# Dilated attention in a written order on three engines, value products of two blocks merged, gate and up interleaved by slice: two layers of a hybrid decoder on one core

## The chip, the core and the metric

The kernel runs on one core of one Trainium2 chip. The time is the device time of one execution in microseconds (us). The figure compared is the median of several runs. Beside these there is one profiled execution, from which every row of the trace below comes; rows name lines of the kernel before the change (L1090 is its line 1090).

## The reference, cut to what matters

Two decoder layers over 512 positions of width 1024, all in float32. Each layer is a half-step SwiGLU, a token mixer and another half-step SwiGLU; every one of these six sub-layers sits between two RMS norms with shift, scale and gate taken from `c`. The mixer of layer 0 is latent attention (MLA, 16 heads, causal in blocks of 128). The mixer of layer 1 is dilated attention: three groups of 16 heads with dilations 1, 4 and 16, whose results are weighted by their log-sum-exps.

```python
def swiglu(h, w_gate, w_up, w_down):
    return (jax.nn.silu(h @ w_gate) * (h @ w_up)) @ w_down
...
for g, (window, dilation) in enumerate(DIL_GROUPS):
    o, lse = strided_window_attention(
        proj[:, :, g, 0], proj[:, :, g, 1], proj[:, :, g, 2],
        dilation, window // dilation, rel_bias[:, g * DIL_HEADS:(g + 1) * DIL_HEADS])
    outs.append(o)
    lses.append(lse)
alpha = jax.nn.softmax(jnp.stack(lses, axis=0), axis=0)
o = jnp.sum(alpha[..., None] * jnp.stack(outs, axis=0).astype(jnp.float32), axis=0)
return o.astype(h.dtype).reshape(B, S, DIL_WIDTH) @ w_o
```

## The kernel before

**Dense products.** Every float32 product with a weight is done as three products of split operands (`mm3`, L143 to L145): a raw weight tile comes by DMA (`raw`, 5 buffers), ScalarE (ACT) rounds it to a high part (`whi`, L128, 6 buffers), VectorE (DVE) subtracts to get the low part (`wlo`, L130, in two halves), and TensorE (PE) adds high*high, high*low and low*high. A weight slice is 128x128; a full moving operand has 512 columns. In the trace one such matmul is one record; a plain float32 matmul (transposes, scores, value products) shows as two records.

**Gate and up.** `gate_up_mm` runs the eight 128-wide slices `k` of the gate product, then the eight of the up product, into two PSUM banks. At the start of a sub-layer the first three units (`head`) run on half the positions (256 columns), while VectorE, ScalarE and GpSimd still make the slices of the modulated input (`modulate`, L305 to L307).

**MLA.** For each pair of heads `c` and block `i`, `score`, `turn` (transposes, L890) and `weigh` (value products, L904) pass through a pipe: in one step the kernel emits the scores of block i, the transposes of block i-2 and the value products of block i-3. Other products (`BESIDE`) fill the steps.

**Dilated stage.** `Dil.rest` works on eight pairs of heads. While pair p is attended, the nine projection tiles of pair p+1 (`tile`, 24 matmuls each) run, in the order `ORDER`; their place n = 0 to 8 counts the slots of a pair. In the slots stand:

- n = 0 to 3: `scores(p, n)`. Scores contract over 64 rows: the two heads of a pair use the two halves of the array's rows at once (L1090), each into its own bank. VectorE adds the bias, takes row minima and empties the bank (`tensor_tensor_reduce`, L1103).
- after n = 3: `tops` sends minima through DRAM to bring them into another order; at n = 4, `exps` takes all exponentials on ScalarE (L1155), then `norm` and `norm_out` send the sums through DRAM (L1182 to L1188).
- n = 6 to 8 and n = 0, 1 of the next pair: `mix`, that is `turn` of step 0 to 3 (PE transposes at L1210 with copies on VectorE at L1214; step 3 is a transpose on VectorE, L1206) and `weigh` of the step before. `weigh` (L1235) gives each head 64 of the array's columns; at its last step VectorE multiplies by the reciprocal sums (L1245).
- after each value tile: its transposes (`later`, L1065, copy at L1067) one slot on.

There are two pools of four PSUM banks: `mm` for dense products and scores, `aux` for transposes and value sums.

**What sets the order.** The code records operations; outside a `manual_schedule` block a scheduler of the tile layer places each engine's instructions by readiness and priority. Inside `manual_schedule(engines=...)` the named engines keep the order in which the code is written. In the dilated stage before, only its last part is written by hand (PE and DVE). Each engine runs its queue in order.

Of the kernel before, what the change touches and what calls it, by code (L numbers as in the profile page):

```python
# [7 lines left out]
F32 = mybir.dt.float32  # L8
# [4 lines left out]
PE, ACT, DVE, SP = (getattr(mybir.EngineType, n) for n in ("PE", "Activation", "DVE", "SP"))  # L13

P = 128
SEQ = 512
# [6 lines left out]
PART = 3  # L23
# [9 lines left out]
SPARE = (2, 3)  # L33
TURN = 26
START = 4
HT = SEQ // 2
TT = SEQ // P

# [482 lines left out]
class Ffn:  # L521
# [178 lines left out]
class Mla(Mixer):  # L700
# [148 lines left out]
    def attend(self, c, i, pipe):  # L849
# [48 lines left out]
        def weigh(i):  # L898
            if i == 0:
                box["o"] = t.bank("aux")  # L900
            for j in range(i + 1):
                for e in range(2):
                    h = 2 * c + e
                    nc.tensor.matmul(  # L904
                        box["o"][64 * e : 64 * e + 64, i * P : (i + 1) * P],
                        self.v[j, h // 8][:, (h % 8) * 64 : (h % 8) * 64 + 64],
                        box[i][e][:, j * P : (j + 1) * P],
                        start=i == j == 0,
                        stop=i == j == 3,
                        skip_group_check=True,  # L910
                    )
            if i == 3:
                self.put_o(box["o"])

        pipe.push(i, score, turn, weigh)

# [26 lines left out]
class Dil(Mixer):  # L943
# [124 lines left out]

            self.later = turn

    def scores(self, p, u):
        t, nc = self.t, self.t.nc
        if u == 0:
            self.pairs.pop(p - 2, None)
            self.pairs[p] = {
                "bias": [self.bias_of(2 * p + e) for e in range(2)],
                "m": t.tmp.tile([P, 3, 4, 2], F32, tag="dm", name="dm", bufs=2),
                "z": t.tmp.tile([P, 3, 4, 2], F32, tag="dz", name="dz", bufs=2),
                "y": {},
            }  # L1080
# [3 lines left out]
        s = [t.bank() for _ in range(2)]  # L1084
        y = [t.t("sq", SB) if u < 2 else t.t("u", UB) for _ in range(2)]
        at = 0
        for i, k0, n, b0 in blocks:
            for e in range(2):
                rows = slice(64 * e, 64 * e + 64)
                nc.tensor.matmul(  # L1090
                    s[e][:, at : at + n],
                    q[rows, i * P : (i + 1) * P],
                    k[rows, k0 : k0 + n],
                    start=True,
                    stop=True,
                )
            at += n
        for e in range(2):
            pair["y"][u, e] = y[e]
            at = 0  # L1100
            for i, k0, n, b0 in blocks:
                c = slice(at, at + n)
                nc.vector.tensor_tensor_reduce(  # L1103
                    y[e][:, c],
                    s[e][:, c],
                    pair["bias"][e][:, b0 : b0 + n],
                    -0.125,
                    3e38,
                    ALU.add,
                    ALU.min,  # L1110
                    accum_out=pair["m"][:, g, i, e : e + 1],
                )
                at += n
        if u == 3:
            self.tops(pair)

    def natural(self, dram, src):

# [2 lines left out]
        for a in range(4):  # L1121
            nc.sync.dma_start(
                dram[1].rearrange("(l a j) v -> a l j v", a=4, j=4)[a], src[32 * a : 32 * a + 32, 2]
            )

    def tops(self, pair):
        t, nc = self.t, self.t.nc
        m = pair["m"]
        m0 = t.dram.tile([2, SEQ, 2], F32, tag="m0", name="m0", bufs=2)
        t0 = t.dram.tile([SEQ, 2], F32, tag="t0", name="t0", bufs=2)  # L1130
        self.natural(m0, m)
        x = t.tmp.tile([P, 2, 4, 2], F32, tag="x4", name="x4", bufs=2)
        nc.sync.dma_start(x, m0.rearrange("g (p r) v -> p g r v", r=4))
        top = t.tmp.tile([P, 3, 4, 2], F32, tag="y4", name="y4", bufs=2)
        nc.vector.tensor_tensor(top[:, 1], x[:, 0], x[:, 1], ALU.min)
        nc.vector.tensor_tensor(top[:, 1], top[:, 1], m[:, 1], ALU.min)
# [5 lines left out]
            )  # L1142
        pair["top"] = top

    def exps(self, p):
        nc = self.t.nc
        pair = self.pairs[p]
        for u, (g, blocks) in enumerate(self.BLOCKS):
            for e in range(2):
                y = pair["y"][u, e]  # L1150
                at = 0
                for i, k0, n, b0 in blocks:
# [8 lines left out]
                        accum_out=pair["z"][:, g, i, one],  # L1161
                    )
                    at += n
        self.norm(pair)
        if p < 7:
            self.norm_out(pair)

    def norm(self, pair):
        t, nc = self.t, self.t.nc
# [26 lines left out]
    )  # L1196

    def turn(self, p, step):
        t, nc = self.t, self.t.nc
        _, tag, pieces, _ = self.TURNS[step]  # L1200
        y = self.pairs[p]["y"]
        out = self.pairs[p][step] = []
        for e in range(2):
            x = t.t(tag)
            if pieces is None:
                nc.vector.transpose(x, y[3, e])  # L1206
            else:
                b = t.bank("aux")
                for c, (u, j) in enumerate(pieces):
                    nc.tensor.transpose(  # L1210
                        b[:, c * P : (c + 1) * P], y[u, e][:, j * P : (j + 1) * P], t.ident
                    )
                n = len(pieces) * P
                nc.vector.tensor_copy(x[:, :n], b[:, :n])  # L1214
            out.append(x)

    def weigh(self, p, step, first=0, last=3):
        t, nc = self.t, self.t.nc
# [26 lines left out]
            nc.vector.tensor_tensor(x, pair["acc"], pair["r"], ALU.mult)  # L1245
            self.of.append(x)

    def mix(self, p, step):
        if step < 4:
            self.turn(p, step)  # L1250
        if step:
            self.weigh(p, step - 1)

    def rest(self):
        t = self.t
        t.gates(self)
        self.of = []
        self.tables()
        for u in self.ORDER[6:]:
            self.tile(0, u, 0, SEQ)  # L1260
# [24 lines left out]
        for x in self.of[PART:]:  # L1285
            self.put_o(x)
        self.exps(7)
# [128 lines left out]
```

## Time and profile before

| what | value |
|---|---|
| median of 3 runs | 2275.35 us (2274.54 to 2275.74) |
| the profiled execution | 2273.08 us, its span 2271.3 us |
| busy share of the span: PE, DVE, ACT, POOL | 99%, 53%, 38%, 5% |
| latent attention, 446 to 582 us: busy PE, DVE, ACT | 134.58, 92.02, 100.92 us of 136.00 |
| one pair of the dilated stage, mean of three: busy PE, DVE, ACT | 62.25, 25.52, 24.35 us |

The profiled execution is 2.27 us (0.1%) below the median. Rows of the timeline give start, duration, engine, line, operation, output and inputs, shape (rows*columns of the array, then the moving operand), and count. Matmuls overlap in the pipeline, so durations of neighbours overlap too: what one costs is the distance from its start to the next start.

### The profile page before, as it was taken

How to read it: one execution, taken by the hardware profiler on the slowest of the kernel's cores; microseconds unless marked ns; L12 is line 12 of the kernel's file. 1: busy time of each engine (PE TensorE's matmuls, PEld its weight loads, DVE VectorE, ACT ScalarE, POOL GpSimd, SP SyncE). 2: the span in 40 equal slices, each digit the busy share in tenths (PEclk: the TensorE clock that was granted, in tenths of full speed). 3: DMA queues.
4: the chain of work that ended last, by engine and by line, in shares of the span. 5: the costliest groups of instructions: out<-in, count | busy, mean ns of one | idle time of the engine just before them, and what ended most of it. 6: DMA issues, size and time to landing. Idle time of an engine off the chain costs nothing. (4 is left out here: it accounts for less than half of the span.)

```text
span 2271.3 us, 30190 instructions
## 1 busy us (share of the span) xinstructions
PE 2240.5 (99%) x11422; PEld 1851.4 (82%) x11422; DVE 1203.6 (53%) x2712; ACT 861.3 (38%) x1752; POOL 105.2 (5%) x143
## 2 busy tenths in 40 slices
PE   7999999999999999999999999999999999999998
PEld 5888888877898888898888888778878878888887
DVE  7666566677655366474554473334434367243344
ACT  4422135577633132353222352444344346332232
POOL 0000001210110000020000010000000002000000
PEclk9999999999999999999999999999999999999999
DMA  8575662311255365344653523333333332243231
GB/s 307 163 249 180 187 232 68 100 48 57 76 171 180 93 213 173 106 140 127 191 174 114 156 93 105 80 96 87 81 93 87 89 79 80 75 130 100 76 111 38
DMA packets 121224, 284.04 MB, mean 125 GB/s; under 512 B 44130, under 2 KB 48501, under 8 KB 121078
## 3 DMA queue, kind: packets, MB, share of 16 engines
q1 hardware_dynamic: 121078, 282.11, 40.8%
q8 instruction: 89, 1.46, 0.3%
q14 instruction: 57, 0.47, 0.1%
HBM read 279.67 MB, written 2.39 MB: 124 GB/s over the span
## 5 line engine op out<-in xcount | busy, mean ns | idle before, releaser
L143 PE MATMUL mm<-s,whi 128*128 128x512 f32 (+1 forms) x2116 | 796.9, 377 | 3.5 <-ACT whi L128 2.4
L144 PE MATMUL mm<-s,whi 128*128 128x512 f32 (+1 forms) x2116 | 790.9, 374 | 0.0
L145 PE MATMUL mm<-s,wlo 128*128 128x512 f32 (+1 forms) x2116 | 790.5, 374 | 0.0
L128 ACT ACTIVATE whi<-raw 128x1024 fp32r<-128x1024 f32 (+1 forms) x356 | 369.7, 1053 | 962.2 <-PE mm L144 446.6
L130 DVE TENSOR_TENSOR wlo<-raw,whi 128x512 fp32r<-128x512 f32 (+1 forms) x712 | 465.6, 693 | 397.8 <-ACT whi L128 393.8
L143 PEld LDWEIGHTS mm<-s,whi 128*128 128x128 f32 x2116 | 398.7, 188 | 83.4 <-issue 7.0
L145 PEld LDWEIGHTS mm<-s,wlo 128*128 128x128 f32 x2116 | 398.7, 188 | 70.9
L144 PEld LDWEIGHTS mm<-s,whi 128*128 128x128 f32 x2116 | 398.9, 188 | 68.1
L143 PE MATMUL mm<-whi,s 128*128 128x512 f32 x848 | 332.4, 392 | 1.8 <-ACT s L694 1.1
L144 PE MATMUL mm<-wlo,s 128*128 128x512 f32 x848 | 330.4, 390 | 0.0
L145 PE MATMUL mm<-whi,s 128*128 128x512 f32 x848 | 330.1, 390 | 0.0
L165 DVE CUSTOM_DVE_ANT_0 raw<-raw,cs 128x1024 f32<-128x1024 f32 x130 | 159.9, 1234 | 117.7 <-DMA raw<-w_mod 117.2
L143 PEld LDWEIGHTS mm<-whi,s 128*128 128x128 f32 x848 | 159.2, 188 | 36.3 <-issue 2.5
L145 PEld LDWEIGHTS mm<-whi,s 128*128 128x128 f32 x848 | 159.2, 188 | 33.4 <-issue 0.3
L144 PEld LDWEIGHTS mm<-wlo,s 128*128 128x128 f32 x848 | 159.3, 188 | 32.6 <-issue 0.3
L569 DVE TENSOR_TENSOR gg<-silu,mm 128x512 f32<-128x512 f32 (+1 forms) x95 | 60.3, 635 | 171.5 <-PE mm L145 168.3
L459 DVE TENSOR_TENSOR s<-mm,s 128x512 f32<-128x512 f32 x112 | 76.5, 689 | 125.8 <-PE mm L145 125.6
L318 POOL TENSOR_TENSOR mv<-mv,mhalf 128x1 f32<-128x1 f32 x48 | 36.0, 752 | 1498.0 <-DVE mv L317 1495.5
L570 ACT ACTIVATE s<-gg 128x512 fp32r<-128x512 f32 (+1 forms) x97 | 57.4, 591 | 62.0 <-DVE gg L569 62.0
L567 ACT ACTIVATE silu<-mm 128x512 f32<-128x512 f32 (+1 forms) x95 | 51.5, 543 | 31.9 <-PE mm L145 31.9
L1055 ACT ACTIVATE s<-mm 128x512 f32<-128x512 f32 (+3 forms) x156 | 46.2, 373 | 34.8 <-PE mm L145 34.8
L463 ACT ACTIVATE s<-mm 128x512 f32<-128x512 f32 x40 | 23.8, 595 | 85.8 <-PE mm L145 85.5
(168 smaller groups left out, 1737.3 us busy)
## 6 DMA issues: line engine op xcount, KB each, us to landing
raw<-w_gu SPq DMA_DIRECT2D x168, 512.0 KB, 4.3
raw<-w_mod SPq DMA_DIRECT2D x130, 512.0 KB, 4.8
raw<-w_down SPq DMA_DIRECT2D x88, 512.0 KB, 4.3
raw<-dil_in SPq DMA_DIRECT2D x70, 512.0 KB, 3.6
s<-w_mod SPq DMA_DIRECT2D x28, 256.0 KB, 6.3
raw<-w_gu SPq DMA_DIRECT2D x16, 256.0 KB, 3.6
raw<-mla_o SPq DMA_DIRECT2D x8, 512.0 KB, 3.7
raw<-dil_o SPq DMA_DIRECT2D x8, 512.0 KB, 3.6
```

The lines of the kernel that those rows point to most:

```text
L128: self.nc.scalar.activation(hi, raw, AF.Copy)
L130: self.nc.vector.tensor_tensor(lo[:, r], raw[:, r], f(hi[:, r]), ALU.subtract)
L143: mm(out, w[0], m[0], start=first, stop=False)
L144: mm(out, w[0], m[1], start=False, stop=False)
L145: mm(out, w[1], m[0], start=False, stop=last)
L165: nc.vector.tensor_tensor_reduce(raw, raw, self.cs, 1.0, 0.0, ALU.mult, ALU.add, accum_out=t[:, 0:1])
L318: nc.gpsimd.tensor_tensor(v[:, 1:2], v[:, 0:1], self.mhalf[:, 0:1], ALU.pow)
L459: nc.vector.tensor_tensor(y, b, y, ALU.add)
L567: nc.scalar.activation(s, banks[0], AF.Silu)
L569: nc.vector.tensor_tensor(v, s, banks[1], ALU.mult)
L570: nc.scalar.activation(ghi, v, AF.Copy)
L1055: nc.scalar.activation(out, src, AF.Copy)
```

## The change

- `gate_up_mm` swaps its loops: slice `k` outside, gate and up inside.
- In MLA, `weigh` does nothing for even blocks (but for taking the bank at block 0) and at odd blocks runs the products of the block before and of its own.
- In the dilated stage, PE, ACT and DVE follow the written order. Scores of a pair go into two slots: u = 0 and 1 at n = 0, u = 2 and 3 at n = 1 (u = 3 into `aux` banks). Value products go into the same two slots of the next pair: steps 0 and 1 at n = 0, steps 2 and 3 at n = 1. `turn` is split into the transposes (`turn_up`) and the copies (`turn_down`); steps 0 and 1 are at n = 7 and 8, step 2 at n = 0.
- `tops` is split: the DMAs out and in (`tops_out`) stay with the scores, the VectorE part runs at n = 3. Exponentials are spread over n = 4 to 6, `norm` follows at n = 6, `norm_out` at the end of n = 8. Bias tables are loaded at n = 6 of the pair before.
- `ahead` loads and splits weight tiles `LEAD` = 5 places ahead, the first tiles of the output weights among them.

```diff
+LEAD = 5
...
-        for g in range(2):
-            for k in ks:
+        for k in ks:
+            for g in range(2):
                 t.mm3(
...
             if i == 0:
                 box["o"] = t.bank("aux")
+            elif i % 2:
+                for q in (i - 1, i):
+                    products(q)
+            if i == 3:
+                self.put_o(box["o"])
+
+        def products(i):
             for j in range(i + 1):
...
-    def exps(self, p):
+    def exps(self, p, us):
...
+    def slot(self, p, n):
+
+        if n == 0:
+            if p:
+                b = self.turn_up(p - 1, 2)
+                self.values(p - 1, (0, 1))
+            self.scores(p, 0)
+            self.scores(p, 1)
+            if p:
+                self.turn_down(p - 1, 2, b)
+                self.turn(p - 1, 3)
+        elif n == 1:
+            if p:
+                self.values(p - 1, (2, 3))
+            self.scores(p, 2)
+            self.scores(p, 3, "aux")
+        elif n == 6:
+            self.biases(p + 1)
+        elif n > 6:
+            self.turn(p, n - 7)
+
+    def beside(self, p, n):
+        if n == 3:
+            self.tops(self.pairs[p])
+        elif n == 4:
+            self.exps(p, (2,))
+        elif n == 5:
+            self.exps(p, (0, 1))
+        elif n == 6:
+            self.exps(p, (3,))
+            self.norm(self.pairs[p])
...
-        for p in range(7):
-            for n, u in enumerate(self.ORDER):
-                if n < 4:
-                    self.scores(p, n)
-                if n < 2 and p:
-                    self.mix(p - 1, 3 + n)
-                if n == 4:
-                    self.exps(p)
-                if n >= 6:
-                    self.mix(p, n - 6)
-                if p == 6 and n == 8:
+        with t.tc.manual_schedule(engines={PE, ACT, DVE}):
+            for at, (p, u) in enumerate(tiles):
+                n = self.ORDER.index(u)
+                if p:
+                    self.slot(p - 1, n)
+                if (p, n) == (7, 8):
                     self.scores(7, 0)
-                self.tile(p + 1, u, 0, SEQ)
+                self.ahead(at + LEAD)
+                if p:
+                    self.beside(p - 1, n)
+                self.tile(p, u, 0, SEQ)
+                if p and n == 8:
+                    self.norm_out(self.pairs[p - 1])
         self.later()
+        b = self.turn_up(6, 2)
+        self.values(6, (0, 1))
+        self.turn_down(6, 2, b)
+        self.turn(6, 3)
         self.scores(7, 1)
         for x in self.of[:PART]:
             self.put_o(x)
-        self.mix(6, 3)
         t.new_y()
-        for j in range(PART):
-            self.out_weights(j)
         self.scores(7, 2)
-        self.mix(6, 4)
+        self.values(6, (2, 3))
         self.scores(7, 3)
+        self.tops(self.pairs[7])
```

The order of instructions, at three places. First PE at slot n = 0 of a pair in the dilated stage, before (L1065 are transposes of a value tile, L1090 scores, L1235 value products, L143 to L145 the projection tiles):

```order
L145 MATMUL mm<-s,wlo 128x512
L1065 MATMUL aux<-ident,s 128x128 x4
L1090 MATMUL mm<-s 128x128 x2
L1090 MATMUL mm<-s 128x256 x2
L1235 MATMUL aux<-silu,s 64x128 x8
L143 MATMUL mm<-s,whi 128x512
L144 MATMUL mm<-s,whi 128x512
```

The same place after the change (lines of the changed kernel: L1071 value transposes, L1218 transposes of exponentials, L1252 value products, L1096 scores, L144 to L146 the tiles):

```order
L146 MATMUL mm<-s,wlo 128x512
L1071 MATMUL aux<-ident,s 128x128 x4
L1218 MATMUL aux<-ident,u 128x128 x8
L1252 MATMUL aux<-silu,s 64x256 x4
L1252 MATMUL aux<-gg,s 64x256 x2
L1252 MATMUL aux<-gg,s 64x128 x2
L1096 MATMUL mm<-s 128x128 x2
L1096 MATMUL mm<-s 128x256 x6
L144 MATMUL mm<-s,whi 128x512
```

The scores of u = 1 and the value products of steps 0 and 1 have come into this slot from n = 1, 7 and 8, and step 2's value products have left it for n = 1.

Second PE in MLA between two steps, before (L862 scores, L890 transposes, L904 value products):

```order
L145 MATMUL mm<-whi,s 128x512
L862 MATMUL mm<-s 128x512 x2
L890 MATMUL aux<-ident,u 128x128 x4
L904 MATMUL aux<-silu,s 64x128 x2
L862 MATMUL mm<-s 128x128 x2
L890 MATMUL aux<-ident,sq 128x128 x6
L904 MATMUL aux<-gg,s 64x128 x4
L143 MATMUL mm<-s,whi 128x512
```

and after (L863, L891 and L912 are the same three):

```order
L146 MATMUL mm<-whi,s 128x512
L863 MATMUL mm<-s 128x512 x2
L891 MATMUL aux<-ident,u 128x128 x4
L863 MATMUL mm<-s 128x128 x2
L891 MATMUL aux<-ident,sq 128x128 x6
L912 MATMUL aux<-silu,s 64x128 x2
L912 MATMUL aux<-gg,s 64x128 x4
L144 MATMUL mm<-s,whi 128x512
```

The products of the even block have moved behind the next step's scores and transposes, to those of the odd block.

Third DVE ahead of slot n = 0 after the change (L1073 is the copy of a value tile, L1192 to L1194 are `norm_out`, L1109 empties the score banks, each reduction followed by the reading of its minimum):

```order
L1073 COPY s<-aux 128x512
L1192 TENSOR_TENSOR w_13075<-x_12934 128x4x2
L1193 TENSOR_TENSOR w_13075<-w_13075,dz 128x4x2
L1194 RECIPROCAL w_13075<-w_13075 128x8
L1109 ISA sq,dm<-mm,s 128x128
L1109 ISA dm 128x1
L1109 ISA sq,dm<-mm,s 128x256
```

Before, these three stood ahead of a STREAM_TRANSPOSE, copies and splits of weights, which came before the reductions; now the reductions of slot 0 are directly behind them.

More of the change, by code (lines that the diff above doesn't have):

```diff
@@ L1075, in scores @@
             self.pairs[p] = {
[L1076 removed]
+                "bias": self.bias.pop(p),
                 "m": t.tmp.tile([P, 3, 4, 2], F32, tag="dm", name="dm", bufs=2),
@@ L1083, in scores @@
         q, k = self.qkv[p, 3 * g], self.qkv[p, 3 * g + 1]
-        s = [t.bank() for _ in range(2)]
+        s = [t.bank(tag) for _ in range(2)]
         y = [t.t("sq", SB) if u < 2 else t.t("u", UB) for _ in range(2)]
@@ L1114, in scores, with biases @@
         if u == 3:
-            self.tops(pair)
+            self.tops_out(pair)
+    def biases(self, p):
+        self.bias[p] = [self.bias_of(2 * p + e) for e in range(2)]
     def natural(self, dram, src):
@@ L1246, in weigh, with values, ahead @@
             self.of.append(x)
[L1248 to L1252, printed above, removed]
+    def values(self, p, steps):
+        for n in steps:
+            self.weigh(p, n)
+    def ahead(self, n):
+        while self.coming and self.ahead_of < n:
+            p, u = self.coming.pop(0)
+            self.ahead_of += 1
+            if p == "out":
+                self.out_weights(u)
+            else:
+                self.wt[p, u] = self.t.weights(self.t.a["dil_in"][p, u])
+    def slot(self, p, n):
[27 more added lines that the diff above has]
+            self.norm(self.pairs[p])
     def rest(self):
```

65 lines of the change are left out of this document (36 added, 29 removed).

## The prediction

> **What bounds the kernel now.** I read the page first, then PE's waits, then the timeline of PE in the stages that the change touches.
>
> ```profile
> PE 2240.5 (99%) x11422; PEld 1851.4 (82%) x11422; DVE 1203.6 (53%) x2712; ACT 861.3 (38%) x1752; POOL 105.2 (5%) x143
> ```
>
> PE is busy in 99% of the span. So time can go only if PE waits less or if its own stream becomes shorter. The waits:
>
> ```profile
> PE mm L377 <- DVE s L371: 5.3, 4, 3.3
> PE mm L143 <- DVE dm L1103: 0.7, 1, 0.7
> ```
>
> The longest, 5.3 us, is in the first 20 us, which the change hardly touches. The only wait on the score reductions in the whole run is one of 0.7 us, after the last pair. The next rows are windows, with the busy times of PE, weight load, DVE, ACT and POOL, the granted clock, and the DMA: MLA, then one pair of the dilated stage:
>
> ```profile
> 446.00:582.00 136.00, 134.58 (x842) 99.00 (x840) 92.02 (x281) 100.92 (x239) 16.62 (x23) 1.00 0.16 48
> 1546.44:1608.64 62.20, 62.20 (x347) 49.70 (x346) 25.48 (x83) 24.36 (x76) 0.35 (x2) 1.00 0.35 89
> ```
>
> The pair takes 62.20 us, PE is busy in all of it at the full clock, DVE in 25.48, ACT in 24.36. Written order on DVE and ACT can therefore win nothing there by itself; what counts is what PE's stream costs. "Busy" does not say that the stream is dense, so I look at the distance from start to start. First a slot with scores alone, then one with transposes alone:
>
> ```profile
> 1539.14 0.39 PE L144 MATMUL mm<-s,whi 128*128 128x512 f32 x1
> 1539.37 0.39 PE L145 MATMUL mm<-s,wlo 128*128 128x512 f32 x1
> 1539.68 1.16 PE L1090 MATMUL mm<-s 64*128 64x128 f32 x16
> 1540.78 0.50 PE L143 MATMUL mm<-s,whi 128*128 128x512 f32 x1
> 1541.11 0.39 PE L144 MATMUL mm<-s,whi 128*128 128x512 f32 x1
> ...
> 1563.77 0.40 PE L145 MATMUL mm<-s,wlo 128*128 128x512 f32 x1
> 1564.00 1.08 PE L1210 MATMUL aux<-ident,sq 128*128 128x128 f32 x8
> 1564.84 0.48 PE L143 MATMUL mm<-s,whi 128*128 128x512 f32 x1
> 1565.15 0.40 PE L144 MATMUL mm<-s,whi 128*128 128x512 f32 x1
> ```
>
> A dense matmul takes 0.23 us (1539.14 to 1539.37). From the last one before the scores to the second one after them are 1.74 us; without the scores it would be two steps, 0.46. The 16 score records cost 1.28. They run two by two, one head on each half of the rows, so they are 8 steps of 128 columns. The 8 transposes, also 8 steps of 128 columns but on the whole array (128*128), cost 1565.15 - 1563.77 - 0.46 = 0.92. So a block of work with 64 rows costs 0.36 us more than the same steps on the whole array. The neighbours show where: 0.31 instead of 0.23 from L145 to L1090, and 0.33 from L143 to L144 after it. **Changing the shape in which the array is used costs time on each side.** The tail of the stage gives a second price, from blocks that follow each other:
>
> ```profile
> 1838.94 1.16 PE L1090 MATMUL mm<-s 64*128 64x128 f32 x16
> 1840.03 1.09 PE L1235 MATMUL aux<-gg,s 128*64 128x128 f32 x16
> 1841.06 1.16 PE L1090 MATMUL mm<-s 64*128 64x128 f32 x16
> ```
>
> Score blocks (64*128) and value blocks (128*64) in a chain take 1.09 and 1.03 us, with one change each in place of two: 1.28 - 1.06 = 0.22 per change. From the other side 0.36 / 2 = 0.18. I take 0.20 us per change, with 0.18 and 0.23 as bounds.
>
> [...]
>
> **The change part by part.** *Dilated stage.* Going through PE's order before and after, I count the places where it passes between whole array, 64 rows and 64 columns: 113 before, 57 after. Per pair: before, n = 0 and 1 hold scores and value products (3 changes each), n = 2 and 3 scores alone, n = 7 and 8 value products alone (2 each), 14 in all; after, only n = 0 and 1 (3 each). Eight fewer in seven pairs make the 56. The same number of matmuls runs. 56 x 0.20 = **11.2 us less** (10.1 to 12.9).
>
> *MLA.* Value products stand between whole-array work; the scores there use 96 rows. Two steps, without and with value products:
>
> ```profile
> 451.95 0.39 PE L145 MATMUL mm<-s,wlo 128*128 128x512 f32 x1
> 452.18 1.45 PE L862 MATMUL mm<-s 96*128 96x384 f32 x4
> 453.47 0.38 PE L890 MATMUL aux<-ident,sq 128*128 128x128 f32 x2
> 453.61 0.47 PE L143 MATMUL mm<-whi,s 128*128 128x512 f32 x1
> 453.93 0.39 PE L144 MATMUL mm<-wlo,s 128*128 128x512 f32 x1
> ...
> 482.70 0.40 PE L145 MATMUL mm<-s,wlo 128*128 128x512 f32 x1
> 484.22 0.38 PE L890 MATMUL aux<-ident,sq 128*128 128x128 f32 x2
> 484.53 1.09 PE L904 MATMUL aux<-gg,s 128*64 128x128 f32 x16
> 485.56 0.50 PE L143 MATMUL mm<-whi,s 128*128 128x512 f32 x1
> 485.89 0.39 PE L144 MATMUL mm<-wlo,s 128*128 128x512 f32 x1
> ```
>
> 3.19 - 1.98 = 1.21 us for 16 value records, again 8 steps: 0.29 above the transposes, 0.15 per change at the least. L145 to L862 takes the plain 0.23, so 96 rows count as the whole array. 32 blocks of value products become 18, 28 changes go: 28 x 0.20 = **5.6 us less** (4.1 to 6.4). Products of even blocks come one step later and keep their transposed operand (`silu`, two buffers) longer; the copies that need the buffer wait for PE products which stand right behind the transposes, and are used two steps later, so I put that at nothing; ACT and DVE are busy 74% and 68% there (100.92 and 92.02 of 136), and the cost if that cover is short is below, with the first rival.
>
> *The new slot n = 0.* Here four `mm` banks fill at once, and the next tile wants the first of them again. Before, one tile lay between two score pairs. DVE empties a bank thus:
>
> ```profile
> 1838.02 0.42 DVE L1103 CUSTOM_DVE_ANT_0 sq<-mm,s 128x256 f32<-128x256 f32 x1
> 1838.37 0.08 DVE L1103 DVE_READ_ACCUMULATOR2_ANT dm<- 128x1 f32 x1
> ...
> 1842.23 0.29 DVE L1103 CUSTOM_DVE_ANT_0 u<-mm,s 128x128 f32<-128x128 f32 x1
> 1842.44 0.29 DVE L1103 CUSTOM_DVE_ANT_0 u<-mm,s 128x128 f32<-128x128 f32 x1
> ```
>
> A step takes 0.35 us for 256 columns and 0.21 for 128; the first bank holds one of each, 0.56, and 0.1 for the last read: 0.65. PE's part: u = 0 is 2 + 4 steps of 128 columns, u = 1 is 8 more, 0.11 each (0.92 / 8), with a change ahead and behind 1.5 + 0.2 = 1.7 us to the next tile. The first bank is written after some 5 steps and a matmul's 0.4 of latency (the durations shown), about 1.0, and free at 1.65. It is a close race: 0 to 0.1 us per pair if DVE comes at once. Behind these reductions DVE has two copies and two transposes (0.6 each) for products that run a tile later. I take 0.5 us for seven pairs (0 to 2).
>
> *Other moves.* Exponentials spread over three slots lie beside tiles of 24 x 0.23 = 5.5 us each; ACT then does at most one weight split, 8 exponentials and the emptying of a tile in a slot, and a late emptying hurts only after three more tiles have taken banks. Weight DMAs are issued as far ahead as the buffers allow in both. Bias loads move ahead of use. All beside PE: nothing.
>
> *Tail.* Transposes and products of step 2, 0 and 1 of pair 6 leave n = 7 and 8 and stand behind the last tile. There DVE, not PE, sets the pace: PE's 0.7 us of waiting on it, quoted first, ends that chain. DVE gets two copies and two transposes more in that stretch, 4 x 0.6, and `norm_out`'s 0.5: the wait is over 2.9 us later counted from the last tile, which itself ends some 2.6 us earlier because the work left. And one change fewer in the chain wins nothing there. **0.6 us more** (0 to 1.5).
>
> *Slice-major gate and up.* In steady state the same matmuls at the same pitch; both banks are ready together, and the next unit but one needs them 11 us later. At a sub-layer's start PE waits for slices:
>
> ```profile
> 983.72 0.42 DVE L307 TENSOR_TENSOR s<-u,s 128x256 fp32r<-128x256 f32 x1
> 984.19 0.39 PE L144 MATMUL mm<-s 128*128 128x256 f32 x1 [0.19 <-DVE s L307]
> ```
>
> PE goes on when the low half of the last slice lands. In both orders 47 matmuls stand between the head's first and that one, so the interleaving lets PE wait later, not less: **0** (2 us either way, the four waits of such a start being 1.3 us here).
>
> Sum: -11.2 - 5.6 + 0.5 + 0.6 = -15.7. Against the profiled execution (span 2271.3, with 1.8 us around it 2273.1) that is 2257.4; the median before, 2275.35, is 2.3 us above that, so I predict 2275.35 - 15.7 = **2259.6 us** (-0.7%).
>
> **Rivals.** *Emptying eats part of it.* If a DVE operation of 0.65 us stands in the way at both slots of each pair, PE waits 14 x 0.65 = 9 us, and 2268.7 remains. For it: the race above is close. Against it: in the written order nothing but three small operations stands directly ahead of the reductions. [...] MLA's ACT, at 74%, would have the same effect on a smaller scale.
>
> *The price is not one of changes.* If the 0.3 us belong to each block's first records whatever stands before, merging keeps most of them; with the two costs above 2274 to 2277 results. Against it: blocks in a chain are cheaper, 1.06 against 1.28.
>
> *Slower.* `norm_out` now stands directly ahead of the reductions of slot 0 in DVE's queue and waits for sums that go through DRAM; a late sum would hold the reductions, the banks and so PE.
>
> ```profile
> 1442.70 0.19 ACT L1155 ACTIVATION_READ_ACCUMULATOR u<-u,y 128x1 f32 x1
> 1449.04 0.17 DVE L1182 TENSOR_TENSOR w<-x 128x8 f32<-128x8 f32 x1 [1.32 <-DMA x<-z]
> ...
> 1397.17 5.82 SPq L981 DMA_DIRECT2D s<-tv  x12
> ```
>
> That way took 6.2 us before. After, exponentials end in the tile of n = 6, and `norm_out` is wanted some 14 us later. With the twelve bias loads (5.8 us of issuing) now ahead in the queue it is 12. It decides from 14 us on; at 18 us PE would lose 4 us in each of seven pairs, and the time would be 2259.6 + 28 = 2287.6.
>
> **How the numbers follow.** The forecast (2254 to 2264) gets 0.70, emptying 0.15 (2264 to 2270), no price of changes 0.08, slower 0.07. The forecast's bounds are 10.1 + 4.1 - 2 - 1.5 and 12.9 + 6.4 less nothing, with up to 2 us from the starts: -8.7 to -21.3 at the extremes, hardly all at once. The range 2254 to 2268.5 holds the forecast and most of the first rival, about 0.8. By over 0.2% (4.6 us, about what a measurement can tell from no change): faster 0.85, same 0.08, slower 0.07.
>
> **What would show it.** One pair of the dilated stage near 60.5 us in place of 62.2, PE still busy in all of it, and slots n = 2, 3, 7 and 8 without a 64-wide block; MLA 5 us shorter. A wait of PE's tile (the mm3 after the scores) on the reductions would show the first rival, DVE waiting on x<-z the last one. I am wrong if the pair is shorter by clearly more or less than 1.6 us with no wait of PE in it, for then the price is not what I read.

## The result and the profile after

| | before | after |
|---|---|---|
| median | 2274.95 us (2274.54 to 2275.74, 4 runs) | 2260.96 us (2258.17 to 2261.21, 4 runs) |
| the profiled execution | 2273.08 us, its span 2271.3 | 2258.17 us, its span 2256.1 |

The ratio is 0.9935, with a 95% interval of 0.9918 to 0.9953: 14.0 us less (10.7 to 18.7). The forecast was 15.7 less (2259.6). Rows of after name its own lines; what they are called before is said where it matters.

First the page of after, its line of busy times, and the rows of PE's waits that answer to those of before (engine, what waits, what for; us in total, times, longest):

```profile
PE 2224.4 (99%) x11422; PEld 1853.9 (82%) x11422; DVE 1196.9 (53%) x2712; ACT 848.9 (38%) x1752; POOL 107.9 (5%) x143
```

```profile
PE mm L378 <- DVE s L372: 5.3, 4, 3.3
...
PE mm L144 <- DVE dm L1109: 1.6, 1, 1.6
...
PE mm L144 <- ACT s L695: 1.2, 1, 1.2
```

The same 11422 matmuls now keep PE busy for 16.1 us less, at the same 99%. What went was not waiting but length of PE's own stream. The one wait on the score reductions (L1109, before L1103) has grown from 0.7 to 1.6 us; it is still a single one, at the tail, and none stands in a slot.

Then windows of after: MLA, and two pairs of the dilated stage (columns as in the prediction):

```profile
446.00:577.00 131.00, 129.30 (x826) 98.44 (x826) 91.39 (x280) 99.93 (x239) 16.78 (x24) 1.00 0.16 49
1506.01:1566.47 60.46, 60.46 (x347) 50.08 (x346) 25.40 (x83) 24.29 (x75) 0.20 (x1) 1.00 0.35 90
1566.47:1626.93 60.46, 60.46 (x347) 50.08 (x346) 25.39 (x83) 24.29 (x75) 0.20 (x1) 1.00 0.37 98
```

A pair takes 60.46 us; the prediction asked for "near 60.5 us in place of 62.2, PE still busy in all of it". Slot n = 0 in the timeline of after, PE and then DVE:

```profile
1513.98 1.08 PE L1252 MATMUL aux<-silu,s 128*64 128x256 f32 x8
1514.89 0.82 PE L1252 MATMUL aux<-gg,s 128*64 128x256 f32 x8
1515.64 1.79 PE L1096 MATMUL mm<-s 64*128 64x128 f32 x16
1517.36 0.50 PE L144 MATMUL mm<-s,whi 128*128 128x512 f32 x1
1517.70 0.39 PE L145 MATMUL mm<-s,whi 128*128 128x512 f32 x1
```

```profile
1516.60 0.29 DVE L1109 CUSTOM_DVE_ANT_0 sq<-mm,s 128x128 f32<-128x128 f32 x1 [2.17 <-PE mm L1096]
1516.82 0.08 DVE L1109 DVE_READ_ACCUMULATOR2_ANT dm<- 128x1 f32 x1
1516.82 0.42 DVE L1109 CUSTOM_DVE_ANT_0 sq<-mm,s 128x256 f32<-128x256 f32 x1
1517.16 0.08 DVE L1109 DVE_READ_ACCUMULATOR2_ANT dm<- 128x1 f32 x1
```

Value products, then scores, then the next tile, in one go. The race for the first score bank is as close as the prediction reckoned: the bank is empty at 1517.16 + 0.08 = 1517.24, and PE asks for it at 1517.36. It is won by 0.12 us, with no wait.

To find where the rest of the time went I divide each trace at records that all kernels have: the first score of MLA, the first transposes of the sub-layer behind it, the first score and the last value product of the dilated stage, the end. Every stretch is the difference of two starts in the trace (us). The last column is the mean period of five pairs, taken at the transposes of value tiles. Taken at the first scores of the pairs it is 62.22 before and the same 60.46 after, because the order before shifts a little from pair to pair.

| kernel | to MLA | MLA | middle | dilated | rest | pair |
|---|---|---|---|---|---|---|
| before | 447.65 | 156.87 | 796.06 | 468.01 | 402.67 | 62.17 |
| after | 447.95 | 152.62 | 796.04 | 456.41 | 403.07 | 60.46 |
| e1_slice | 447.98 | 158.44 * | 796.04 | 467.87 | 402.34 | 62.16 |
| e2_mla | 448.85 * | 154.26 * | 796.05 | 468.28 | 403.60 | 62.24 |
| e3_dil | 447.55 | 158.50 * | 796.05 | 456.41 | 402.19 | 60.46 |
| e4_four_visits | 447.86 | 154.19 * | 796.06 | 462.43 | 403.53 | 61.31 |
| e5_alternate | 448.06 | 154.23 * | 796.06 | 460.68 | 402.58 | 61.18 |
| e6_tail | 449.09 * | 154.22 * | 796.07 | 456.24 | 403.36 * | 60.46 |
| e7_last_pair | 447.81 | 154.54 * | 796.06 | 456.40 | 403.05 | 60.46 |
| e9_copies_first | 448.19 | 154.20 * | 796.06 | 461.41 | 402.61 | 61.28 |
| e10_norm_early | 447.88 | 154.24 * | 796.06 | 459.02 * | 403.21 * | 60.46 |
| e11_mla_cover | 447.80 | 152.92 | 796.04 | 458.04 * | 402.91 | 60.46 |
| e12_turn3_first | 449.17 * | 154.20 * | 796.03 | 458.02 | 403.02 | 60.73 |
| e13_tail_order | 447.86 | 154.17 * | 796.06 | 454.34 | 402.66 | 60.46 |

So the change took 4.25 us from MLA and 11.60 from the dilated stage; the start, the middle and the rest moved by 0.7 together, up. The middle repeats within 0.04 us in all kernels, and the dilated stage within 0.01 us in those that share its code in the written order (e3_dil, e7_last_pair). Stretches with a star hold some 3.4 us at half clock; at MLA they come and go with the same code. Windows of before and of e3_dil, whose code up to there is the same (the third number from the end is the granted clock):

```profile
449.00:453.00 4.00, 4.00 (x18) 3.25 (x19) 1.61 (x8) 3.97 (x12) 0.95 (x2) 1.00 0.32 127
```

```profile
449.00:453.00 4.00, 4.00 (x12) 3.20 (x13) 1.62 (x8) 3.83 (x11) 0.85 (x2) 0.57 0.29 111
```

In 449 to 453 us before ran 18 matmul records at clock 1.00, e3_dil 12 at 0.57. The step from the second to the third score of MLA is 1.5 to 1.6 us longer in all eleven profiles with a star at MLA, and equal to 0.01 us in the three others. I subtract that step where I compare MLA.

### The profile page after: what moved, and what is told of

Read it like the earlier page. It is cut to its first block, busy times and chain, and to the rows that moved or that the text cites. A ratio compares the mean times of both kernels' runs of the same rounds, so it can differ in the third digit from the quotient of the medians.

```text
span 2256.1 us, 30214 instructions
## 1 busy us (share of the span) xinstructions
PE 2224.4 (99%) x11422; PEld 1853.9 (82%) x11422; DVE 1196.9 (53%) x2712; ACT 848.9 (38%) x1752; POOL 107.9 (5%) x143
## 4 chain that ended last, share of the span: by engine, by line
PE 92%; issue 2%; ACT 2%; DVE 2%; DMA 1%; POOL 1%; SPq 0%; POOLq 0%; DVEq 0%; ACTq 0%
PE mm L144 28%; PE mm L145 28%; PE mm L146 28%; PE mm L863 1%; PE aux L1252 1%; PE mm L1096 1%; PE aux L1218 1%; PE aux L912 1%; POOL mv L319 1%; PE aux L891 1%; PE aux L513 1%; PE aux L1071 0%; ACT whi L129 0%; DVE x L500 0%; DMA d<-w 0%
## 5 line engine op out<-in xcount | busy, mean ns | idle before, releaser
L144 PE MATMUL mm<-s,whi 128*128 128x512 f32 (+1 forms) x2116 | 793.9, 376 | 2.7 <-ACT whi L129 2.4
L146 PE MATMUL mm<-s,wlo 128*128 128x512 f32 (+1 forms) x2116 | 790.0, 373 | 0.0
L145 PE MATMUL mm<-s,whi 128*128 128x512 f32 (+1 forms) x2116 | 790.0, 373 | 0.0
L144 PEld LDWEIGHTS mm<-s,whi 128*128 128x128 f32 x2116 | 398.4, 188 | 77.4 <-ACT whi L129 3.1
L146 PEld LDWEIGHTS mm<-s,wlo 128*128 128x128 f32 x2116 | 398.6, 188 | 70.8
L145 PEld LDWEIGHTS mm<-s,whi 128*128 128x128 f32 x2116 | 398.9, 189 | 68.7
L144 PE MATMUL mm<-whi,s 128*128 128x512 f32 x848 | 332.4, 392 | 2.8 <-DVE dm L1109 1.6
L145 PE MATMUL mm<-wlo,s 128*128 128x512 f32 x848 | 330.5, 390 | 0.0
L146 PE MATMUL mm<-whi,s 128*128 128x512 f32 x848 | 330.1, 389 | 0.0
L144 PEld LDWEIGHTS mm<-whi,s 128*128 128x128 f32 x848 | 159.2, 188 | 37.0 <-issue 2.9
L146 PEld LDWEIGHTS mm<-whi,s 128*128 128x128 f32 x848 | 159.2, 188 | 33.3 <-issue 0.2
L145 PEld LDWEIGHTS mm<-wlo,s 128*128 128x128 f32 x848 | 159.2, 188 | 32.9 <-issue 0.5
L145 PE MATMUL mm<-s 128*128 128x256 f32 (+1 forms) x176 | 52.9, 306 | 3.9 <-DVE s L308 2.3
```

The lines of the kernel that those rows point to most:

```text
L144: mm(out, w[0], m[0], start=first, stop=False)
L145: mm(out, w[0], m[1], start=False, stop=False)
L146: mm(out, w[1], m[0], start=False, stop=last)
```

## The experiments

**e1_slice, e2_mla, e3_dil: each part alone.**

```diff
 e1_slice: before, and
-        for g in range(2):
-            for k in ks:
+        for k in ks:
+            for g in range(2):
 e2_mla: before, and
+            elif i % 2:
+                for q in (i - 1, i):
+                    products(q)
 ...
 e3_dil: after, with both of these put back
```

> The kernel before with the slice-major order of gate and up alone. Theory (the three places of the change act apart, and this one does nothing): within 0.3 us of the kernel before, and the anchors at the four FFN heads (first down products of each stage) unmoved by more than 0.3 us. Rival (the waits of TensorE at the FFN heads are those for the last slices, and this order shortens them): 2 us shorter.

Measured: 2274.45 us against 2272.96 of before on that chip, ratio 1.0004 (0.9995 to 1.0012). But for the half clock, no stretch moves by more than 0.33 us; the middle takes 796.04 against 796.06. In the start the 0.33 us is real: from the 200th to the 300th matmul record of the run PE takes 22.67 us in the three kernels with the old order of gate and up and 22.93 to 22.97 in the eleven with the new one, because two steps near 73 us take 0.35 and 0.34 in place of 0.23. Why they do is open. So this order costs 0.3 us there and gains nothing that shows. (Within 0.3 us was too narrow for a median, since the half clock alone is worth 1.6.)

> The kernel before with the value products of two blocks merged in the MLA stage alone. Theory (the price is one of changes of array shape, 28 fewer, at 0.17 to 0.20 us each): 4.0 to 5.6 us shorter, nearer the lower end because the last pair now waits for its second block; the period of a head pair 0.7 us shorter, the end of MLA as much earlier as the whole kernel. Rival (the 4 us that the whole change showed in this stage came from elsewhere, from the earlier gate and up): within 0.5 us of the kernel before.

Measured: 2272.36 us, ratio 0.9991 (0.9983 to 1.0000): 0 to 3.9 us less. By the median alone this run would look like the rival. Its trace says otherwise: MLA 154.26 us, of which 1.57 is half clock; without it 4.18 less than before, as in the changed kernel (4.25). A second stretch at half clock, ahead of MLA (400 to 410 us, granted 0.83), cost the profiled execution another 1.2. Whether the timed runs had both more often than those of before is not shown.

> The changed kernel with the gate and up order and the MLA stage put back as before, so that the dilated stage alone differs from before. Theory (the terms add): 11.0 to 11.5 us shorter than before, the pair period 1.6 to 1.7 us shorter, MLA unmoved. Rival (the parts interact, because the dilated stage starts earlier or later against its weight loads): less than 10 or more than 12.5 us.

Measured: 2263.11 us, ratio 0.9955 (0.9943 to 0.9968), 7.3 to 13 us less. The medians are 9.9 apart, which by itself is just under the rival's 10; the interval holds both. In the trace the dilated stage takes 456.41 us, to the hundredth what it takes in the changed kernel, 11.60 less than before; MLA differs by the half clock alone. **The parts add (11.60 + 4.18 against 15.85), and two of the three make all of the gain.**

**e4_four_visits, e5_alternate: is it the changes of array shape?** Both keep the written order on three engines and every operation; they only put changes of shape back.

```diff
 e4_four_visits: after, and in slot n
-  n = 0: scores(p, 0), scores(p, 1)     n = 1: scores(p, 2), scores(p, 3, "aux")
+  n = 0 to 3: scores(p, n); tops one slot later, exps (2, 0, 1) at n = 5
 e5_alternate: after, and in slot 0 (slot 1 likewise with 2 and 3)
-                self.values(p - 1, (0, 1))
-            self.scores(p, 0)
-            self.scores(p, 1)
+                self.values(p - 1, (0,))
+            self.scores(p, 0)
+            if p:
+                self.values(p - 1, (1,))
+            self.scores(p, 1)
```

> The changed kernel, but the four score blocks of a pair stand in four slots (one block each) in place of two, with the column maxima and the exponentials as much later as they must be; the order is still written by hand, and the value products stay in two places. That adds two visits per pair, 28 changes of array shape over seven pairs. Theory (the gain is one of changes): 4.7 to 6.1 us longer than the changed kernel (28 x 0.17 to 0.22), the pair period 0.7 to 0.9 us longer. Rival (the gain comes from the written order and from the exponentials and tile loads that it spreads): within 0.5 us of the changed kernel.

Measured: 2265.58 us, ratio to before 0.9965 (0.9953 to 0.9977). A pair in its window:

```profile
1497.67:1558.97 61.30, 61.30 (x348) 49.90 (x347) 25.39 (x83) 24.07 (x77) 0.20 (x1) 1.00 0.37 91
```

PE is still busy throughout, in a period that is 61.31 - 60.46 = 0.85 us longer for 4 changes more: 0.21 each. The whole stage is 462.43 - 456.41 = 6.02 us longer for 28: 0.215 each. The theory's upper end; the rival (written order, spread of the exponentials) falls.

> The changed kernel, but in the first two slots of a pair the value products of one block and the scores of one block alternate (values, scores, values, scores in place of values twice, scores twice). PE still goes from the whole array and back once per slot, and has two more changes straight from the one half shape to the other in each slot: 4 per pair, 24 over the six pairs that have both. Theory (every change of shape has its price, 0.21 us in this stage): 5.0 us longer than the changed kernel, the pair period 0.85 us longer. Rival (the price is one of leaving the whole array and coming back to it): the pair period unchanged within 0.1 us. Between them, if a change straight from half to half costs only its entry or its exit (0.09 us as the step behind such a change shows it): 2 us.

Measured: 2264.69 us, ratio 0.9960 (0.9946 to 0.9974); the period 0.72 us longer (61.18, with PE busy in all of it), the stage 4.27. That is 0.18 for each change straight from 64 columns to 64 rows or back, a little less than a change from or to the whole array. Returning to the whole array is not what costs: these changes, which skip it, cost nearly as much (0.18 against 0.21).

**e9_copies_first, e12_turn3_first: how much room has the bank race?**

```diff
 e9_copies_first: after, and in slot 0
+            if p:
+                self.turn_down(p - 1, 2, b)
+                self.turn(p - 1, 3)
             self.scores(p, 0)
             self.scores(p, 1)
-            if p:
-                self.turn_down(p - 1, 2, b)
-                self.turn(p - 1, 3)
 e12_turn3_first: only turn(p - 1, 3) moved ahead
```

> The changed kernel, but in the first slot of a pair the copies of turn 2 and the transposes of turn 3 (four VectorE operations of some 0.65 us, 2.6 us in all) are written ahead of the two score blocks, so that the reductions that empty the score banks come 2.6 us later. Theory of the prediction (the banks are needed again so soon that a delay of 2.4 us costs 0.5 us per pair): the pair period 0.3 to 0.6 us longer, 2 to 3 us in all. Rival (as the changed kernel shows no wait of PE on a reduction in any slot, the banks have room to spare): the pair period unchanged within 0.1 us.

Measured: 2265.02 us, ratio 0.9962 (0.9947 to 0.9977); the period 61.28, 0.82 us longer, the stage 5.00. The first of these rows is of the waits within the pairs, the others of its timeline:

```profile
PE mm L144 <- DVE dm L1109: 4.5, 6, 0.8
```

```profile
1518.97 1.29 DVE L1232 STREAM_TRANSPOSE gg<-u 128x512 f32<-128x512 f32 x2
1520.19 0.25 DVE L1109 CUSTOM_DVE_ANT_0 sq<-mm,s 128x128 f32<-128x128 f32 x1
...
1520.86 0.50 PE L144 MATMUL mm<-s,whi 128*128 128x512 f32 x1 [0.75 <-DVE dm L1109]
```

The prediction had 0.5 us for all pairs, not for each, so the expectation overstated it. Here is the first rival of the prediction, brought about: the tile waits 0.75 us on the reductions, in each of six pairs. "Room to spare" falls.

> The changed kernel, but in the first slot of a pair only the two transposes of turn 3 on VectorE (1.3 us) are written ahead of the score blocks; the copies of turn 2 stay behind. Theory (the copies-first run lost 0.82 us per pair for 2.6 us of delay, so that the score banks have 1.8 us to spare): the pair period unchanged within 0.1 us. Rival (any delay of the reductions costs in proportion): 0.4 us per pair, 2.5 us in all.

Measured: 2261.91 us, ratio 0.9948 (0.9933 to 0.9963); the period 60.73, 0.27 us longer, the stage 1.61, with a wait of 0.2 per pair. Between the two expectations, and nearer the rival. The reading of 1.8 us of room was wrong, and the rows above say why: the room is the 0.12 us of the race, and DVE's 2.17 us of idleness ahead of the reductions hides part of what is put there, as far as its own inputs let it start; that last part is a reading, which no run takes apart. In e9_copies_first DVE waits 0.66 us for the value products (L1252) before its copies begin, at 1517.77.

**e7_last_pair, e11_mla_cover: why MLA gave 4.25 and not more.** From the last score of one pair of heads to the last of the next, the first six pairs gain 0.67 to 0.73 us each, for 4 changes: 0.17 per change. The seventh and the last have only 2 changes fewer (36 changes are left of 64 in the traces). The seventh loses 0.2 us instead of gaining, and the last gains 0.3.

```diff
 e7_last_pair: after, and
+            if c == 7:
+                products(i)
             elif i % 2:
 e11_mla_cover: after, and
+            if c == 6 and i > 1:
+                products(i)
             elif i % 2:
```

> The changed kernel, but the last pair of heads of the MLA stage weighs each block by itself again, as before the change; the other seven pairs stay merged. Theory (in the last pair the merge costs more by its waits for the second block, some 0.9 us, than its four changes of shape save, 0.7): the end of the MLA stage 0.1 to 0.3 us earlier than in the changed kernel. Rival (the last pair's loss has another source, such as the slices that follow it): 0.7 us later.

Measured: 2260.30 us, ratio 0.9942 (0.9927 to 0.9957). MLA 154.54 us, less 1.63 at half clock: 0.29 us longer than after. Neither number came. The last pair's merge does save, 0.29 us for its 2 changes; the loss does not lie in it.

> The changed kernel, but in the seventh of the eight pairs of heads of MLA the blocks 2 and 3 are weighed one by one, as before the change. Theory (the changed kernel loses some 0.8 us at the first score block of the last pair because the value products of the seventh pair's block 2, which stood there before between the scores and the transposes, were moved behind: there is nothing left that hides the softmax chain): the step from the first to the second score block of the last pair 0.8 us shorter, a visit more (0.35 us), the end of MLA 0.4 to 0.5 us earlier. Rival (the loss has to do with the slices or the banks there): the end of MLA 0.35 us later.

Measured: 2260.90 us, ratio 0.9944 (0.9927 to 0.9960); MLA 152.92 us with no half clock, 0.30 longer, near the rival's 0.35, and the step in question equal to 0.03 us (5.08 and 5.05). The theory falls: blocks 2 and 3 of the seventh pair only pay for their visit. These two runs price a change in MLA directly: 2 more cost 0.29 and 0.30 us, 0.15 each. What the timeline of after has at that step:

```profile
547.33 0.85 PE L891 MATMUL aux<-ident,sq 128*128 128x128 f32 x6 [0.19 <-DVE sq L874]
548.11 0.44 PE L912 MATMUL aux<-silu,s 128*64 128x128 f32 x4
548.32 0.69 DVE L893 COPY gg<-aux 128x512 f32<-128x512 f32 x1
548.48 0.50 PE L144 MATMUL mm<-whi,s 128*128 128x512 f32 x1
549.06 0.66 PE L912 MATMUL aux<-gg,s 128*64 128x128 f32 x8
```

The value products of blocks 0 and 1 do not stand together: block 1's operand (`gg`) is copied until 549.01, and the scheduler has put a dense matmul in between. PE waits 0.19 for the scaled scores, and after that one dense matmul it starts nothing until the copy ends. So this one visit is still two, and waits besides. Before, PE came to this chain later, having its visits still to pay. That DVE sets the pace there is how I read these rows; no run took the copy earlier.

**e6_tail, e10_norm_early, e13_tail_order: the tail.** The part products of the last sub-layer begin 11.30 us after the last tile's end (1815.94 to 1827.24), before 7.64. Rows of after, DVE and PE:

```profile
1824.36 0.69 DVE L696 TENSOR_TENSOR s<-s 128x512 fp32r<-128x512 f32 x1
...
1825.17 0.69 DVE L696 TENSOR_TENSOR s<-s 128x512 fp32r<-128x512 f32 x1
...
1825.98 0.69 DVE L696 TENSOR_TENSOR s<-s 128x512 fp32r<-128x512 f32 x1
...
1827.24 0.47 PE L144 MATMUL mm<-whi,s 128*128 128x512 f32 x1 [1.59 <-DVE dm L1109]
...
1828.52 0.69 DVE L1262 TENSOR_TENSOR s<-aux,s 128x512 f32<-128x512 f32 x1 [0.59 <-issue]
```

```diff
 e6_tail: after, and
                 if (p, n) == (7, 8):
                     self.scores(7, 0)
+                    for x in self.of[:PART]:
+                        self.put_o(x)
 ...
-        for x in self.of[:PART]:
-            self.put_o(x)
         t.new_y()
 e10_norm_early: e6_tail, and norm_out(pairs[6]) right behind scores(7, 0)
 e13_tail_order: norm_out as in e10_norm_early, but put_o at (p, n) == (7, 6)
```

> The changed kernel, but the first three normed outputs of the dilated stage are split into their halves beside the last tile, and not between the last reductions. Theory (the 1.6 us that the last FFN's first products wait on a reduction come from the three low halves of 0.69 us that stand ahead of that reduction on VectorE): the first product of the last FFN stands 1.5 to 1.7 us earlier, with no wait ahead of it, and so do the last value product and the end. Rival (another late row takes its place, the product with the reciprocal that comes 0.6 us late, or the exponentials of the last pair): 0.0 to 0.7 us earlier at the last value product.

Measured: 2257.11 us, ratio 0.9931 (0.9916 to 0.9946). Timeline of e6_tail:

```profile
1828.34 0.50 PE L144 MATMUL mm<-whi,s 128*128 128x512 f32 x1
...
1831.56 0.69 DVE L1262 TENSOR_TENSOR s<-aux,s 128x512 f32<-128x512 f32 x1 [2.67 <-DMA s<-d]
...
1833.15 0.50 PE L144 MATMUL mm<-whi,s 128*128 128x512 f32 x1 [0.41 <-DVE dm L1109]
```

The first product comes without a wait, 1828.34 - 1818.70 = 9.64 us after the last tile: 1.66 earlier, as the theory said. But the stage ends only 0.17 earlier (456.24 against 456.41), as the rival said. The product with the reciprocal now waits 2.67 us for the DMA that spreads the sums, the last reductions stand behind it, and PE waits 0.41 us for those. With 0.3 more that it waits later on for exponentials, this is about half of what was lost again; the rest stands in no row of waits. One late row had covered another.

> The run with the early low halves (e6_tail), and besides the reciprocal of the seventh pair's sums is written ahead of the last tile and not behind it. Theory (with the lows gone, the product with the reciprocal waits 2.67 us for the DMA that spreads it, the last reductions stand behind it on VectorE, and that took back what the first products had gained): the wait of the product is gone or under 0.5 us, the last value product and the end of that stage 1.2 to 1.8 us earlier than in the changed kernel. Rival (the chain of the last pair's maxima and sums through DRAM sets the end whatever stands ahead): within 0.4 us of the changed kernel at the last value product.

Measured: 2259.00 us, ratio 0.9939 (0.9924 to 0.9953); the stage 459.02 us, 2.61 longer than after. Neither. Some 1.6 of it, by what such a stretch costs in the other profiles, is half clock, which here came in the tail, just behind a wait of 1.20 us (granted clock 0.50 in 1821.8 to 1825.2 us):

```profile
1821.80:1825.20 3.40, 3.40 (x16) 2.71 (x17) 2.18 (x8) 0.55 (x2) 0.00 (x0) 0.50 0.00 0
```

Some 1.0 us is left. The product with the reciprocal is early now, but outside the hand-written block the scheduler chose another order for PE's tail: it puts scores between pieces of the value products, with a change of shape at each, and other scores where a bank is not yet free. The stage has 61 changes of shape in place of 57. Timeline of e10_norm_early:

```profile
1821.24 0.49 PE L1096 MATMUL mm<-s 64*128 64x128 f32 x2 [1.20 <-DVE dm L1109]
...
1827.27 0.43 PE L1252 MATMUL aux<-silu,s 128*64 128x128 f32 x2
1827.63 0.48 PE L1096 MATMUL mm<-s 64*128 64x128 f32 x2
1828.05 0.98 PE L1252 MATMUL aux<-silu,s 128*64 128x128 f32 x13
```

> The changed kernel with both late rows of its tail moved and TensorE's order left as it is: the first three normed outputs are split three tiles earlier (beside the seventh tile of the last round), and the reciprocal of the seventh pair's sums is written ahead of the last tile. In the run before it (e10_norm_early) the scheduler had also put TensorE's tail into another order, so that it did not test the reciprocal. Theory (two late rows, the low halves first and the product with the reciprocal behind them, cost the tail 1.6 us): no wait of TensorE on a reduction in the tail, the product with the reciprocal waits under 0.5 us, and the last value product stands 1.4 to 1.7 us earlier against the last tile than in the changed kernel. Rival (the chain of the last pair through DRAM sets the end): within 0.4 us of the changed kernel there.

Measured: 2256.76 us (2255.36 to 2257.43), ratio 0.9921 (0.9908 to 0.9935): faster than before, and the lowest median of all. Timeline of e13_tail_order:

```profile
1826.52 0.50 PE L144 MATMUL mm<-whi,s 128*128 128x512 f32 x1
...
1826.92 0.69 DVE L1262 TENSOR_TENSOR s<-aux,s 128x512 f32<-128x512 f32 x1
```

Neither row waits. The stage takes 454.34 us, 2.07 less than after, and the last value product stands 2.07 earlier against the last tile. The theory holds in kind, and the gain is above the 1.4 to 1.7 expected. In the stage, which repeats within 0.01 us in kernels that share its code, 2.07 is clear; medians 4.2 us apart, taken at different times, would not settle a difference of 2.

## Why the prediction was right, step by step

**The price of a change of shape: right in kind.** Forecast 0.20 us with bounds of 0.18 and 0.23. The count was right: the traces show 113 and 57 changes in the dilated stage, 64 and 36 in MLA. In the dilated stage the period fell by 62.17 - 60.46 = 1.71 for 8 changes, 0.214 each (0.22 by the first scores); e4_four_visits gave 0.215. In MLA it was 0.17 in the first six pairs and 0.15 in e7_last_pair and e11_mla_cover, near the lower price that the row there had shown (0.15 at the least). The step that failed is to carry 0.20 from one stage to the other: the term of 5.6 should have been some 28 x 0.17 = 4.8. Why value products cost less in MLA is open.

**MLA: 5.6 forecast, 4.25 measured.** 0.8 of the difference is the price. The other 0.5 is the seventh pair, which should have gained 0.34 and lost 0.2; by the rows above, because the operand of block 1 is late, which no run tested. The sentence that failed put the later products "at nothing", on the ground that copies are used two steps later. That fits the other pairs, where PE had other work; there it had run out.

**Dilated stage: 11.2 forecast, about 12 measured** (56 x 0.214), of which the tail gave back some 0.4, so that 11.60 remain.

**Slot n = 0: 0.5 forecast, nothing measured.** The working was right (free after 1.65, needed at 1.7; in the trace 1.60 and 1.72 from the first score), and the 0.5 a margin for DVE coming late, which it did not. That the danger was real, e9_copies_first shows: the same operations, written four lines higher, cost 5.0 us.

**Tail: 0.6 forecast, about 0.4 measured,** by the mechanism named: DVE sets the pace (PE waits 1.59 us on one of its reductions). This 0.4 is what is left of the stage, so it is no better known than the price (0.7 if the period is taken at the first scores). Its two parts were both too small: the first product stands 3.66 us later behind the last tile (2.9 forecast), and the last tile ends some 3.4 earlier beside the price of the changes (2.6 forecast). The forecast counted the rows that come in (copies, transposes, `norm_out`); those whose move wins time back are the three low halves, and behind them the reciprocal (e6_tail, e13_tail_order).

**Slice-major order: nothing forecast, 0.3 us longer at the start** (e1_slice).

The errors, +1.35 from MLA against -0.8, -0.5 and -0.2, cancel: the two stages lost 15.85 us where the sum said 15.7. That the sum is closer than its terms is luck. The medians differ by 14.0; how much of the rest is half clock in the timed runs is not shown. The rivals fell for their stated reasons: no wait of PE on a reduction within the pairs, and no price that merging keeps. `norm_out` did not hold the reductions in any pair: ahead of slot 0 DVE waits 2.17 us in each of the six pairs, for PE's scores and not for a DMA.

Each change costs, 0.15 to 0.22 us in these runs; what PE does in that time no run shows. For the 84 changes, 56 x 0.214 and 28 x 0.17 make 16.7 us; the forecast's 0.20 made 16.8.

## What to carry to other kernels

Where PE is 99% busy, look at the distance from start to start around blocks that use part of the array: each change of shape was paid for here (0.15 to 0.22 us), so work of one shape belongs together. When such blocks are gathered, count what must be emptied before the next dense product needs the bank, and put nothing ahead of it on the emptying engine (2.6 us of copies and transposes there cost 0.82 us a pair in e9_copies_first). Before moving one late row in a tail, list the rows that are late behind it, and make sure that the move does not hand the order to the scheduler.

## What the runs showed of the hardware

- Half clock after short waits. In eleven of fourteen profiles PE ran at half clock for some 3.4 us right behind the two waits of 0.64 and 0.78 us at the start of MLA (in e1_slice steps of 0.43 us in place of 0.23, granted 0.83 over 450 to 460 us, that is 2 x 0.17 x 10 = 3.4 us at half clock), for 1.5 to 1.6 us of loss. In three (e2_mla, e6_tail, e12_turn3_first) it also came at 400 to 410 us (granted 0.83 there too). In the tail it followed the wait of 1.6 us in e11_mla_cover (granted 0.83 in 1826 to 1836 us), for another 1.6, and the one of 1.2 us in e10_norm_early (granted 0.50 in 1821.8 to 1825.2 us); it did not follow the wait of 1.6 us in after (granted 1.00 in 1826 to 1836 us). The same code shows it in one profile and not in another (449 to 453 us: granted 1.00 in before, 0.57 in e3_dil); what decides it no run shows. In those eleven, PE thus lost about twice what the rows of waits show at the start of MLA: 1.4 us of waits and 1.5 to 1.6 us behind them. The profiles of before, after and e3_dil also have one at 25 to 30 us (granted 0.66 in before and after; 0.83 over 20 to 30 us in e3_dil), in before and after behind waits of 2.4 and 0.95 us. The start is no longer for it: 447.95 us to MLA in after, 447.86 in e4_four_visits, which was granted 1.00 in 20 to 30 us.
- The matmuls on 96 rows in MLA cost no change (0.23 us from L145 to L862 in the prediction's rows, the plain step), and a change between the two half shapes cost 0.18 us (e5_alternate), not much less than one from or to the whole array (0.21 in the same stage).
